# A transformer kernel's memory projection: products with the weights' leading part first, by blocks of rows in the last step only

## The chip, the cores and the metric

The kernel runs on one core of a Trainium2 chip. The metric is the device time of one execution in microseconds (us). Five engines work side by side, each through its own instructions in order: TensorE (PE, with its weight loads PEld), VectorE (DVE), ScalarE (ACT), GpSimd (POOL) and SyncE (SP, which issues DMAs). They wait for each other by semaphores.

## The reference

The program is a two-layer encoder over 512 rows of width 1024, with a memory of 256 rows. Each layer adds to its state, in this order: half a SwiGLU feed-forward block, a mixer, cross-attention to the memory, and half a feed-forward block again. Layer 0's mixer joins a sparse attention over selected keys with a differential attention; layer 1's is a banded attention. The change sits in the projection that gives the cross-attention its keys and values; the memory's part of it does not depend on the state:

```python
def memory_xattn(h, m, wq, wkv, qg, kg, wo):
    q = rmsnorm((h @ wq).reshape(bsz, seq, M_HEADS, M_DIM), qg)
    k, v = jnp.split(m @ wkv, 2, axis=-1)
    k = rmsnorm(k.reshape(bsz, -1, M_HEADS, M_DIM), kg)
    v = v.reshape(bsz, -1, M_HEADS, M_DIM)
    logits = jnp.einsum('bshd,bmhd->bhsm', q, k).astype(jnp.float32) * M_DIM ** -0.5
    p = jax.nn.softmax(logits, axis=-1).astype(v.dtype)
    ...

for layer in range(DEPTH):
    h = h + 0.5 * swiglu(rmsnorm(h, g), wg, wu, wd)
    h = h + mixer(rmsnorm(h, mix_g), ...)
    h = h + memory_xattn(rmsnorm(h, mg), rmsnorm(mem, sg), wq, wkv, qg, kg, wo)
    h = h + 0.5 * swiglu(rmsnorm(h, g), wg, wu, wd)
```

Here `m` is 256 x 1024 and `wkv` 1024 x 1024: the first 512 columns give the keys, the others the values.

## The kernel before, in words

**Split operands.** A float32 product is made of three products in a shorter format. Each operand is split into a leading part (names ending in h) and the rest (names ending in l); x·w becomes xh·wh + xh·wl + xl·wh, added up in one PSUM bank. For weights, `wload` issues the DMA of 128 x 1024 values (wf), ACT makes wh (L161), and DVE or POOL makes wl = wf - wh (L163). `wshare` says which of the two: in layer 0's memory projection POOL makes every second one, in layer 1 DVE all. There are three buffers of wf and two each of wh and wl.

**The memory projection, `mem_kv`.** It has eight steps k, one for each 128 rows of `wkv`. A step loads the weights, loads 128 x 256 values of the memory (`mem`), makes their parts mh (ACT, L1098) and ml (DVE, L1100; two buffers each), and multiplies (L1104). There are four PSUM banks, `banks[c][i]`, with c the half of the columns (0 the keys, 1 the values) and i the block of 128 memory rows. A step is twelve products: for each i, for each c, the three of a split product. After the last step, each i has its keys copied out (ACT, L1110, qk) and its values split (ACT, L1116, and DVE, L1117, vp); then the keys are normed (`head_norm`, L715 sq, L717 ss, L720, L248 on POOL, L724).

**The weaving.** PE's order is that of the code. The projection is part of a generator `gemm` that runs beside the attention's generator `att`. `weave` lets `att` run to its next `yield`, a number of nanoseconds; it then pulls `gemm` until the numbers that `gemm` has yielded cover that gap. The attention's gaps in layer 0 are 3900 after the transposes of a new pair of heads, 600 after each of the two groups of logits, and 1950 ahead of the products with the values (PV); in layer 1, 4550, 600, 2600, and 600 after PV. `mem_kv` yields 1300 after every six products. So a gap of 600 takes six products. The order of the other engines is set by the tile scheduler, from its own estimate of when each instruction can start.

**The attention's lines.** Transposes of q and k (L766, L785; read by ACT L775, L789, L790 and DVE L776, L791), logits (L812), softmax (DVE L825 adds the bias and takes the maximum, ACT L826 the exponential e), transposes of e (L837; read by ACT L840 and DVE L841), PV (L864), its result (ACT L868 ot, DVE L869), and the scaling by the row sums (transposes L873 of POOL's rb, DVE L874). The differential attention ends with sums of squares (L929), a power on POOL (L248, orr), a transpose of it (L937) and DVE L938. Each finished output is split for the next product (ACT L1327 oh, DVE L1329 ol). The logits, transposes and PV share four PSUM banks with the tag pb; all projections share four with the tag pa.

**What follows, `out_proj`.** It multiplies the attention's outputs by the mixer's `w_out` (L657). Its first four banks are those of `mem_kv`, so each has to be emptied first. They are given back by DVE's additions L670 to the next four, before the attention is over.

Of the kernel before, what the change touches and what calls it, by code (L numbers as in the profile page):

```python
# [23 lines left out]
KB = D // P  # L24
# [85 lines left out]
class Encoder:  # L110
# [976 lines left out]
    def mem_kv(self, pre, mp):  # L1087

        nc = self.nc
        gain = self.col(pre + "mem_src_norm")  # L1090
        banks = [[self.bank("pa") for _ in range(2)] for _ in range(2)]
        for k in range(KB):
            wh, wl = self.wload(self.I[pre + "mem_wkv"][k], 1024)
            m = mp.tile([P, NMEM], F32, name="mem", tag="mem", bufs=2)
            nc.sync.dma_start(m, self.I["memT"][k * P:(k + 1) * P, :])
            g = gain[:, k:k + 1]
            mh = mp.tile([P, NMEM], F32R, name="mh", tag="mh", bufs=2)
            nc.scalar.activation(mh, m, AF.Copy, scale=g)  # L1098
            ml = mp.tile([P, NMEM], F32R, name="ml", tag="ml", bufs=2)
            nc.vector.scalar_tensor_tensor(ml, m, g, mh.bitcast(F32), op0=OP.mult, op1=OP.subtract)  # L1100
            for i in range(2):
                for c in range(2):
                    for n, (a, b) in enumerate(((mh, wh), (mh, wl), (ml, wh))):
                        nc.tensor.matmul(banks[c][i], a[:, i * P:(i + 1) * P], b[:, c * 512:(c + 1) * 512],  # L1104
                                         start=(k == 0 and n == 0), stop=(k == KB - 1 and n == 2))
                yield 1300
        kn, vp = [], []
        for i in range(2):
            t = mp.tile([P, S], F32, name="qk", tag="qk", bufs=self.qkbufs)
            nc.scalar.copy(t, banks[0][i])  # L1110
            kn.append(t)
            t = mp.tile([P, 1024], F32R, name="vp", tag="vp", bufs=self.vbufs)
            t3 = t.rearrange("p (h d) -> p h d", d=256)
            p3 = banks[1][i].rearrange("p (h d) -> p h d", d=P)
            r = self.mem_r[:, i:i + 1]
            nc.scalar.activation(t3[:, :, :P], p3, AF.Copy, scale=r)  # L1116
            nc.vector.scalar_tensor_tensor(t3[:, :, P:], p3, r, t3.bitcast(F32)[:, :, :P], op0=OP.mult, op1=OP.subtract)  # L1117
            vp.append(t)
        for i in range(2):
            self.head_norm(kn[i], [self.mem_epsv[:, i:i + 1]], P, mp)  # L1120
        self.memkv = (kn, vp)
# [458 lines left out]
```

## Time and profile before

| quantity | value |
|---|---|
| median of 3 runs | 2075.65 us (2075.44 to 2077.47) |
| profiled execution | 2077.4 us, of which span 2075.6 us, mean granted clock 0.999 |
| busy share PE, PEld, DVE, ACT, POOL | 99%, 88%, 75%, 55%, 17% |
| `mem_kv` products | layer 0: 555.1 to 594.8 us; layer 1: 1572.9 to 1608.9 us |
| one product (L1104) | 390 ns median; 64 of each of the three kinds |

The times of the profile are in us from the start of the span. In a timeline a row has its start, its duration, the engine, the line, the operation, out<-in, partitions x elements and a count, and in brackets the idle time of the engine before it and what ended that. PE's products overlap: one lasts 0.39 us and the next starts 0.23 us after it.

### The profile page before, as it was taken

How to read it: one execution, taken by the hardware profiler on the slowest of the kernel's cores; microseconds unless marked ns; L12 is line 12 of the kernel's file. 1: busy time of each engine (PE TensorE's matmuls, PEld its weight loads, DVE VectorE, ACT ScalarE, POOL GpSimd, SP SyncE). 2: the span in 40 equal slices, each digit the busy share in tenths (PEclk: the TensorE clock that was granted, in tenths of full speed). 3: DMA queues.
4: the chain of work that ended last, by engine and by line, in shares of the span. 5: the costliest groups of instructions: out<-in, count | busy, mean ns of one | idle time of the engine just before them, and what ended most of it. 6: DMA issues, size and time to landing. Idle time of an engine off the chain costs nothing.

```text
span 2075.6 us, 32512 instructions
## 1 busy us (share of the span) xinstructions
PE 2045.8 (99%) x12834; PEld 1825.3 (88%) x12834; DVE 1564.7 (75%) x2246; ACT 1136.6 (55%) x1701; POOL 361.7 (17%) x319
## 2 busy tenths in 40 slices
PE   8999999999999999999999999999999999999999
PEld 7989897888788889898989899988888888989997
DVE  8959687699676698685889687685668687958676
ACT  6636354556686565362556354454778566626442
POOL 1101003345431110000020000013453122000000
PEclk9999999999999999999999999999999999999999
DMA  7837545222241166573556466444223324647643
GB/s 218 221 113 193 142 115 180 82 87 82 83 137 61 62 184 172 143 192 113 128 158 176 129 182 164 122 126 149 92 82 125 100 72 141 184 122 182 164 120 94
DMA packets 86121, 279.65 MB, mean 135 GB/s; under 512 B 9680, under 2 KB 12880, under 8 KB 85968
## 3 DMA queue, kind: packets, MB, share of 16 engines
q1 hardware_dynamic: 74448, 235.62, 35.3%
q0 software_dynamic: 11520, 41.95, 11.8%
q8 instruction: 101, 1.65, 0.3%
q14 instruction: 52, 0.43, 0.1%
HBM read 271.24 MB, written 6.29 MB: 134 GB/s over the span
## 4 chain that ended last, share of the span: by engine, by line
PE 86%; DVE 9%; ACT 2%; issue 2%; POOL 1%; DMA 1%; SPq 0%; DVEq 0%; ACTq 0%; POOLq 0%
PE ps_pa L468 26%; PE ps_pa L604 10%; PE ps_pa L706 10%; PE ps_pb L604 10%; PE ps_pb L468 9%; PE ps_pa L657 4%; PE ps_pb L812 2%; PE ps_pa L323 2%; PE ps_pa L1254 2%; PE ps_pb L864 1%; PE ps_pa L1104 1%; PE ps_pb L657 1%; PE ps_pb L837 1%; DVE wl L163 1%; PE ps_pa L1023 1%
## 5 line engine op out<-in xcount | busy, mean ns | idle before, releaser
L161 ACT ACTIVATE wh<-wf 128x1024 fp32r<-128x1024 f32 (+2 forms) x211 | 215.3, 1022 | 345.9 <-PE ps_pa L604 122.1
L163 DVE TENSOR_TENSOR wl<-wf,wh 128x1024 fp32r<-128x1024 f32 (+2 forms) x169 | 200.0, 1188 | 32.5 <-ACT wh L161 29.9
L446 ACT ACTIVATE wh<-s 128x1024 fp32r<-128x1024 f32 x108 | 114.9, 1063 | 111.9 <-PE ps_pa L468 33.6
L525 POOL DMA_DIRECT2D s<-l_ffn_wq x40 | 35.4, 885 | 782.8 <-ACT s L524 739.0
L447 DVE TENSOR_TENSOR wl<-s,wh 128x1024 fp32r<-128x1024 f32 x108 | 132.0, 1222 | 44.3 <-ACT wh L446 40.1
L446 ACT ACTIVATE wh<-wf 128x1024 fp32r<-128x1024 f32 x84 | 89.2, 1062 | 105.9 <-PE ps_pa L468 32.6
L163 POOL TENSOR_TENSOR wl<-wf,wh 128x1024 fp32r<-128x1024 f32 x42 | 101.4, 2415 | 137.6 <-ACT wh L161 135.7
L706 PE MATMUL ps_pa<-wh,xh 128*128 128x512 f32 x384 | 122.8, 401 | 0.1
L706 PE MATMUL ps_pa<-wh,xl 128*128 128x512 f32 x384 | 119.4, 392 | 0.0
L706 PE MATMUL ps_pa<-wl,xh 128*128 128x512 f32 x384 | 119.1, 391 | 0.0
L447 DVE TENSOR_TENSOR wl<-wf,wh 128x1024 fp32r<-128x1024 f32 x84 | 102.5, 1220 | 5.5 <-PE ps_pa L323 3.0
L228 POOL TENSOR_TENSOR acc<-acc,sq 128x512 f32<-128x512 f32 (+1 forms) x37 | 53.0, 1433 | 260.7 <-ACT sq L227 259.7
L614 DVE TENSOR_TENSOR dn<-ps_pa,R 128x512 f32<-128x512 f32 x48 | 33.1, 689 | 83.9 <-PE ps_pa L604 83.5
L604 PE MATMUL ps_pb<-hh,wh 128*128 128x512 f32 x352 | 95.5, 389 | 0.0
L604 PE MATMUL ps_pb<-hl,wh 128*128 128x512 f32 x352 | 95.4, 389 | 0.0
L604 PE MATMUL ps_pb<-hh,wl 128*128 128x512 f32 x352 | 95.4, 389 | 0.0
L604 PE MATMUL ps_pa<-hh,wh 128*128 128x512 f32 x328 | 88.9, 390 | 0.0
L604 PE MATMUL ps_pa<-hl,wh 128*128 128x512 f32 x328 | 88.7, 389 | 0.0
L604 PE MATMUL ps_pa<-hh,wl 128*128 128x512 f32 x328 | 88.6, 389 | 0.0
L614 DVE TENSOR_TENSOR dn<-ps_pb,R 128x512 f32<-128x512 f32 x48 | 33.0, 687 | 71.1 <-PE ps_pb L604 70.7
L706 PEld LDWEIGHTS ps_pa<-wh,xl 128*128 128x128 f32 x384 | 72.5, 189 | 15.9
L706 PEld LDWEIGHTS ps_pa<-wl,xh 128*128 128x128 f32 x384 | 72.4, 188 | 15.8
(377 smaller groups left out, 5853.1 us busy)
## 6 DMA issues: line engine op xcount, KB each, us to landing
wf<-l_ffn_wq SPq DMA_DIRECT2D x120, 512.0 KB, 3.8
s<-l_ffn_wq SPq DMA_DIRECT2D x80, 512.0 KB, 4.4
s<-l_ffn_wq POOLq DMA_DIRECT2D x80, 512.0 KB, 7.4
wf<-l_ffn_wd SPq DMA_DIRECT2D x64, 512.0 KB, 4.1
wf<-l_w_in SPq DMA_DIRECT2D x48, 512.0 KB, 3.3
wf<-l_ffn_wd SPq DMA_DIRECT2D x32, 384.0 KB, 3.1
wf<-l_mem_wkv SPq DMA_DIRECT2D x16, 512.0 KB, 3.3
wf<-l_w_out SPq DMA_DIRECT2D x16, 512.0 KB, 3.3
```

Of the source, the lines that this page charges most:

```text
L161: self.leading = nc.scalar.activation(wh[:, sl], w[:, sl], AF.Copy)
L163: eng.tensor_sub(wl[:, sl], w[:, sl], wh.bitcast(F32)[:, sl])
L228: self.summed = (eng or nc.gpsimd).tensor_add(acc[:, :n], acc[:, :n], sq[:, :n])
L323: nc.tensor.matmul(p, w[a][:, k * P:(k + 1) * P], xs[k][c], start=k == order[0] and a == c == 0, stop=k == order[-1] and a == 1)
L446: self.leading = nc.scalar.activation(h, t, AF.Copy)
L447: self.parted = nc.vector.tensor_sub(l, t, h.bitcast(F32))
L468: self.nc.tensor.matmul(bank[:, sl], w[a][:, o:o + P], xs[k][b], start=first and z == a == b == k == 0, stop=z == a == 1 and k == KB // 2 - 1,
L604: self.nc.tensor.matmul(bank, w[a][:, j * P:(j + 1) * P], h, start=j == a == e == 0, stop=j == nb - 1 and (a, e) == ops[-1])
L614: nc.vector.tensor_mul(t, bank, f.R)
L657: nc.tensor.matmul(banks[dd], a[:, o:o + P], parts(k)[b], start=k == first and a is wh and b == 0, stop=k == last and a is wl)
L706: nc.tensor.matmul(banks[i], xs[k][a][:, i * P:(i + 1) * P], w[b][:, kk * 512:kk * 512 + 512], start=k == a == b == 0, stop=k == KB - 1 an ...
L812: nc.tensor.matmul(bank[:, o:o + n], a, b[:, :n], start=c == 0, stop=c == len(ops) - 1)
```

## The change: the order of the products within a step

```diff
-            for i in range(2):
+            lead, rest = ((mh, wh), (ml, wh)), ((mh, wl),)
+            for i, ops in ((0, lead), (1, lead), (0, rest), (1, rest)) if k < KB - 1 else ((0, lead + rest), (1, lead + rest)):
                 for c in range(2):
-                    for n, (a, b) in enumerate(((mh, wh), (mh, wl), (ml, wh))):
+                    for a, b in ops:
                         nc.tensor.matmul(banks[c][i], a[:, i * P:(i + 1) * P], b[:, c * 512:(c + 1) * 512],
-                                         start=(k == 0 and n == 0), stop=(k == KB - 1 and n == 2))
-                yield 1300
+                                         start=k == 0 and a is mh and b is wh, stop=k == KB - 1 and b is wl)
+                if i or len(ops) > 1:
+                    yield 1300 if len(ops) > 2 else 870
```

In steps 0 to 6 the eight products with wh come first, four for each block of rows i, and the four with wl follow. `gemm` yields 870 after each of the three groups of four. The last step goes by blocks of rows, six products and 1300 each, with wl last in each half. The instructions are the same in number and kind on every engine; lines behind 1108 have moved by two (L1104 is L1105 now, L1110 is L1112, L1117 is L1119, L1329 is L1331). Beyond the stretches from `mem_kv` to `out_proj` in the two layers the order on every engine is that of before.

The first place is PE in layer 0 where `mem_kv` hands its banks to `out_proj`: L864 is a PV product, L766 and L785 are the transposes for the next pair of heads. Before:

```order
L1104 MATMUL ps_pa<-wl,mh 128x512
L1104 MATMUL ps_pa<-wh,ml 128x512
L864 MATMUL ps_pb<-pz0h,vp 128x512
...
L766 MATMUL ps_pb<-ident,qk 128x128 x4
L785 MATMUL ps_pb<-ident,qk 128x128 x4
L657 MATMUL ps_pa<-oh,wh 128x512
```

And of the change:

```order
L1105 MATMUL ps_pa<-wl,mh 128x512
L864 MATMUL ps_pb<-pz0h,vp 128x512
...
L766 MATMUL ps_pb<-ident,qk 128x128 x4
L785 MATMUL ps_pb<-ident,qk 128x128 x4
L1105 MATMUL ps_pa<-wh,mh 128x512
L1105 MATMUL ps_pa<-wh,ml 128x512
L1105 MATMUL ps_pa<-wl,mh 128x512
```

The last six products of `mem_kv` (the block i = 1) have moved behind PV and the two sets of transposes, and `out_proj` follows on them directly.

The second place is ACT's order at the same point. Before:

```order
L1110 COPY qk<-ps_pa 128x512
L161 ACTIVATE wh<-wf 128x1024
L1116 ACTIVATE vp<-ps_pa,mem_r 128x4x128
L715 ACTIVATE sq<-qk 128x512
L868 COPY ot<-ps_pb 64x512
L775 CAST qz_3577<-ps_pb 64x512
L789 ACTIVATE kz0h<-ps_pb,gcol 64x512
L790 ACTIVATE kz0h<-ps_pb,gcol 64x512
```

And of the change:

```order
L868 COPY ot<-ps_pb 64x512
L775 CAST qz_3577<-ps_pb 64x512
L789 ACTIVATE kz0h<-ps_pb,gcol 64x512
L790 ACTIVATE kz0h<-ps_pb,gcol 64x512
L1112 COPY qk<-ps_pa 128x512
L161 ACTIVATE wh<-wf 128x1024
L1118 ACTIVATE vp<-ps_pa,mem_r 128x4x128
```

The second half's copy, with a weight's wh and the values behind it, has gone from ahead of the attention's four pieces (ot, qz and two halves of k) to behind them.

The third place is DVE, some 20 us later in layer 0, where `out_proj` empties its first four banks (L670). Before:

```order
L670 TENSOR_TENSOR x<-ps_pa,xr 128x512 x2
L890 RECIPROCAL rc<-rs 128x4
L841 TENSOR_TENSOR pz0l<-ps_pb,pz0h 128x512
L841 TENSOR_TENSOR pz1l<-ps_pb,pz1h 128x384
L670 TENSOR_TENSOR x<-ps_pa,xr 128x512
L841 TENSOR_TENSOR pz2l<-ps_pb,pz2h 128x384
L670 TENSOR_TENSOR x<-ps_pa,xr 128x512
L869 TENSOR_TENSOR x<-ps_pb,ot 64x512
```

And of the change:

```order
L890 RECIPROCAL rc<-rs 128x4
L841 TENSOR_TENSOR pz0l<-ps_pb,pz0h 128x512
L841 TENSOR_TENSOR pz1l<-ps_pb,pz1h 128x384
L841 TENSOR_TENSOR pz2l<-ps_pb,pz2h 128x384
L869 TENSOR_TENSOR x<-ps_pb,ot 64x512
L670 TENSOR_TENSOR x<-ps_pa,xr 128x512 x4
```

All four additions have moved behind L869, which waits for PV through ACT's ot.

## The prediction

> **What bounds the kernel now.** I read the page first (busy time and the chain that ended last), then TensorE's waits over the whole run, then the timelines of PE, POOL, DVE and ACT where the changed loop runs: from 555 to 596 us for layer 0 and from 1573 to 1609 us for layer 1, each with the 25 us behind it.
>
> ```profile
> PE 2045.8 (99%) x12834; PEld 1825.3 (88%) x12834; DVE 1564.7 (75%) x2246; ACT 1136.6 (55%) x1701; POOL 361.7 (17%) x319
> PE 86%; DVE 9%; ACT 2%; issue 2%; POOL 1%; DMA 1%; SPq 0%; DVEq 0%; ACTq 0%; POOLq 0%
> ```
>
> TensorE is busy for 2045.8 of 2075.6 us. The change keeps its 192 products and their sizes, so the time can only move by what PE waits. The waits (us in total, times, longest) that touch the loop and what follows it:
>
> ```profile
> PE ps_pb L837 <- DVE qz L776: 2.5, 2, 2.0
> PE ps_pa L1104 <- POOL wl L163: 1.9, 2, 1.0
> PE ps_pa L1104 <- ACT qk L731: 0.7, 1, 0.7
> PE ps_pa L1104 <- DVE wl L163: 0.5, 1, 0.5
> PE ps_pa L657 <- DVE vp L1117: 0.3, 1, 0.3
> ```
>
> Only the second and the fourth are waits on the weights' rest, wl: three waits of 2.4 us together. More than that, the loop has no wait on wl to give back.
>
> **What the change removes.** The three waits on PE's timeline (start, duration, in brackets the idle time and who ended it):
>
> ```profile
> 557.98 0.39 PE L1104 MATMUL ps_pa<-wh,mh 128*128 128x512 f32 x1
> 559.37 0.50 PE L1104 MATMUL ps_pa<-wl,mh 128*128 128x512 f32 x1 [1.01 <-POOL wl L163]
> 559.71 0.39 PE L1104 MATMUL ps_pa<-wh,ml 128*128 128x512 f32 x1
> ...
> 560.17 0.39 PE L1104 MATMUL ps_pa<-wl,mh 128*128 128x512 f32 x1
> 560.40 0.40 PE L1104 MATMUL ps_pa<-wh,ml 128*128 128x512 f32 x1
> 560.64 0.60 PE L937 MATMUL ps_pb<-ident,orr 128*128 128x128 f32 x4
> ...
> 579.99 0.50 PE L1104 MATMUL ps_pa<-wl,mh 128*128 128x512 f32 x1 [0.90 <-POOL wl L163]
> ...
> 1600.57 0.50 PE L1104 MATMUL ps_pa<-wl,mh 128*128 128x512 f32 x1 [0.55 <-DVE wl L163]
> ```
>
> Products start 0.23 us apart (560.17, 560.40). From 557.98 to 559.37 is 1.39, so 1.16 is lost, and the product behind starts 0.34 later instead of 0.23: a restart costs 0.11. The first wait cost 1.27; the others, by the same 0.15 beside the idle time, 1.05 + 0.11 = 1.16 and 0.70 + 0.11 = 0.81. Each wl would now be wanted eight products (1.8 us) after its step begins rather than one or two, which covers all three. Removed: 3.24 us.
>
> **What it adds: the attention's turns.** The loop is woven with the attention by the numbers it yields. A gap of 600 between two groups of logits now takes four products (0.92 us) where it took six (1.38 us); so the same step ends later in the attention's course, and what PE meets there is met earlier against the other engines. I go through the places in time order; "t" is PE's own time at the place.
>
> *First attention block, L937.* PE would now reach L937 at 560.64 - 1.27 less two products (16 stand ahead of it, not 18): 558.91. Its operand orr comes from POOL:
>
> ```profile
> 538.42 2.37 POOL L163 TENSOR_TENSOR wl<-wf,wh 128x1024 fp32r<-128x1024 f32 x1 [1.30 <-ACT wh L161]
> ...
> 556.94 2.38 POOL L163 TENSOR_TENSOR wl<-wf,wh 128x1024 fp32r<-128x1024 f32 x1
> 559.29 1.00 POOL L248 TENSOR_TENSOR orr<-ov,mhalf 128x4 f32<-128x4 f32 x1
> ...
> 584.13 2.38 POOL L163 TENSOR_TENSOR wl<-wf,wh 128x1024 fp32r<-128x1024 f32 x1 [4.20 <-ACT wh L161]
> ```
>
> orr is behind that very wl and ends at 560.29, plus 0.05 to start as between POOL's 559.32 and PE's 559.37. L937 starts at 560.35, only 0.29 earlier than before, with two products (0.46) still owed: a wait of 1.44, with its restart 1.55, so that the gain of 1.27 becomes a loss of 0.28. Bounds of the added wait: 0 (orr ahead of wl on POOL) to 1.6.
>
> *Transposes of layer 0 after 587 us.* The four rests now stand between the two groups of logits, so the buffer of wl comes free later, and POOL's 2.4 us of splitting start at about the time of DVE's split of the outputs. What that does has a pair of rows:
>
> ```profile
> 539.17 2.17 DVE L1329 TENSOR_TENSOR ol<-x,oh 128x512 fp32r<-128x512 f32 x1
> ...
> 587.67 0.69 DVE L1329 TENSOR_TENSOR ol<-x,oh 128x512 fp32r<-128x512 f32 x1
> ```
>
> The first lay over POOL's row of 538.42 (to 540.79) and ended at 541.34, its last 0.55 alone; the second ran alone. The Trainium skill, SBUF — State Buffer, section "Who interferes with whom", says that a DVE instruction with two SBUF inputs contends with a GpSimd instruction reading SBUF; the rows agree (2.17 against 0.69 us).
>
> The split can be 1.48 us longer, and the softmax's first pass (L825) stands behind it, whose logits' banks the transposes L837 want. Bounds 0 and 1.48; I take 0.8, about the middle, as part of it is DVE's slack.
>
> *Handover to the output projection, layer 0.* The last step's second half (six products) is pushed behind the PV products and the next pair's transposes, and its bank must be emptied before out_proj's fourth bank is written.
>
> ```profile
> 595.83 0.28 PE L864 MATMUL ps_pb<-pz2l,vp 128*128 128x256 f32 x1
> ...
> 596.74 0.48 PE L657 MATMUL ps_pa<-oh,wh 128*128 128x512 f32 x1
> ...
> 598.89 0.39 PE L657 MATMUL ps_pa<-oh,wh 128*128 128x512 f32 x1
> ```
>
> ```profile
> 594.98 0.62 ACT L1110 COPY qk<-ps_pa 128x512 f32<-128x512 f32 x1
> 595.44 1.11 ACT L161 ACTIVATE wh<-wf 128x1024 fp32r<-128x1024 f32 x1
> 596.40 0.73 ACT L1116 ACTIVATE vp<-ps_pa,mem_r 128x512 fp32r<-128x512 f32 x1
> ...
> 597.67 0.58 ACT L868 COPY ot<-ps_pb 64x512 f32<-64x512 f32 x1
> 598.28 0.58 ACT L775 CAST qz<-ps_pb 64x512 fp32r<-64x512 f32 x1
> 598.76 0.68 ACT L789 ACTIVATE kz0h<-ps_pb,gcol 64x512 fp32r<-64x512 f32 x1
> 599.46 0.68 ACT L790 ACTIVATE kz0h<-ps_pb,gcol 64x512 fp32r<-64x512 f32 x1
> ```
>
> ```profile
> 597.16 0.75 DVE L1117 SCALAR_TENSOR_TENSOR vp<-ps_pa,mem_r,vp 128x512 fp32r<-128x512 f32 x1 [0.71 <-ACT vp L1116]
> ```
>
> With t the start of the last PV product: PE reaches the fourth bank at t + 0.91 (595.83 to 596.74) + 6 x 0.23 + 2.15 (596.74 to 598.89) = t + 4.44. ACT has its four attention pieces ahead now: ot starts at t + 0.37 (618.17 to 618.54, below), then 0.61 + 0.48 + 0.70 + 0.70, the copy 0.46, wh 0.96, vp 0.76, and DVE's 0.75 behind: t + 5.79. The wait is 1.35, with its restart 1.46. Bounds 0 and 1.5.
>
> *out_proj's second four banks, layer 0.* The four additions L670 that empty the first four now all stand behind L869 on DVE; before, all four ran ahead of it.
>
> ```profile
> 618.17 0.28 PE L864 MATMUL ps_pb<-pz2l,vp 128*128 128x256 f32 x1
> ```
>
> ```profile
> 618.54 0.58 ACT L868 COPY ot<-ps_pb 64x512 f32<-64x512 f32 x1 [1.81 <-PE ps_pb L864]
> ```
>
> ```profile
> 616.56 0.68 DVE L670 TENSOR_TENSOR x<-ps_pa,xr 128x512 f32<-128x512 f32 x1
> ...
> 619.16 0.68 DVE L869 TENSOR_TENSOR x<-ps_pb,ot 64x512 f32<-64x512 f32 x1 [1.92 <-ACT ot L868]
> ```
>
> From t = 618.17, L869 starts at t + 0.99 and takes 0.68, L670 0.68: the bank is free at t + 2.35. PE wants it at t + 0.91. Wait 1.44, with restart 1.55; bounds 0 and 1.6. The later three banks follow at 0.68 each, three products (0.69) apart.
>
> *Layer 1.* Its first step waits for a bank, and its end for another:
>
> ```profile
> 1576.95 0.50 PE L1104 MATMUL ps_pa<-wh,mh 128*128 128x512 f32 x1 [0.68 <-ACT qk L731]
> ...
> 1613.87 0.51 PE L657 MATMUL ps_pa<-oh,wh 128*128 128x512 f32 x1 [0.28 <-DVE vp L1117]
> ```
>
> The bank of 1576.95 is the fourth; six products now stand ahead of it instead of nine, while ACT's copy comes no earlier: +0.69 (bounds 0 and 0.7). Between two groups of logits and their transposes PE has four products of cover less (0.92), of which the softmax's slack takes a part I cannot see: +0.5 (bounds 0 and 0.92). At the handover ACT has vp and sq (0.73 and one like it) ahead of the last two exponentials, so the transposes wait: +0.5; and the second half's qk, wh and vp stand behind the next group's exponentials, with DVE's own wl ahead of L1117, so the wait of 1613.87 (0.28, in all 0.45) grows. Adding these pieces up in the new order gives about +1.45 net; bounds for the two together -0.45 (it goes) and 2.6.
>
> **Sum.** Removed 3.24. Added in layer 0: 1.55 + 0.8 + 1.46 + 1.55 = 5.36. Layer 1: 0.69 + 0.5 + 1.95 = 3.14. Net +5.3 us: the profiled execution's 2077.4 (span 2075.6) would become 2082.7. That execution lies 1.75 above the median of 2075.65, so the forecast is 2075.65 + 5.3 = **2080.9 us**. With every added term at its lower bound the sum is -3.7, at its upper 1.55 + 1.5 + 1.5 + 1.6 + 0.7 + 0.9 + 2.6 - 3.24 = +7.1; a stretch at the lower clock (below) adds 1.7.
>
> **The rivals.**
>
> *The covers hold.* Only the waits on wl vanish: ACT and DVE drain the banks in time since they too start 3 us earlier. -3.2 and -0.45 give 2072.0 to 2072.4, inside 0.2% (4.15 us, about what a measurement here can tell from no change). For it: ACT is idle 45% of the span. Against: PE is moved nearer to engines whose queue order, not their speed, sets the wait. It decides where POOL's orr and the two handover banks are ready.
>
> *The waits merely change place.* L937's wait takes the place of the first and the layer-1 bank's of the third, and DVE's and ACT's new queue order at the handovers costs half of what I put down (1.5 of 3.0 in layer 0, 0.7 of 1.95 in layer 1): -3.24 + 1.55 + 0.8 + 1.5 + 0.69 + 0.7 = +2.0, so 2077.7: no change that can be told.
>
> *A long wait lowers the granted clock.* After the wait of 2.0 on qz (542.2) PE ran slower:
>
> ```profile
> 542.20:544.20 2.00, 1.99 (x7) 1.71 (x8) 1.97 (x4) 0.48 (x1) 0.00 (x0) 0.58 0.62 234
> 544.20:546.20 2.00, 2.00 (x6) 1.53 (x6) 0.30 (x1) 0.00 (x0) 0.00 (x0) 0.57 0.03 8
> ```
>
> The columns end with the granted clock, 0.58 and 0.57, and the DMA's two: 4 us at 0.575 lose 1.7 us of work. Should two of my waits run together to 2 us (the handover's could), the sum is 5.3 + 1.7 = +7.0: 2082.7. TensorE: Matmul & The Clock Gate in the Trainium skill, Part 1, has the clock fall only after an idle window of about 3.4 us; by it no wait here would do that, and the sum stays. The row, with 2.05 us, speaks against so long a bound.
>
> **How the numbers follow.** New waits outweigh the old ones, 0.50; with the lower clock too, 0.14; waits change place, 0.24; covers hold, 0.12. The first includes sums from +3 on, so slower by over 0.2% gets 0.14 + about 0.46 = 0.60; faster by over 0.2% needs the last case and 0.5 us beyond it: 0.05; within 0.2% the rest, 0.35. The range reaches from 2075.0 (the rival without change, its handover terms near nothing) to 2085.5 (the lower clock and half of the remaining upper bounds); the likeliest case alone spans 2078.5 to 2083.
>
> **What would show it.** Right: no wait of the product line on wl; L937 waiting about 1.4 for POOL's orr; L657 waiting for vp and for x (L670), over 1 us each in layer 0; the fourth bank in layer 1 waiting about 1.4. Every stretch outside 555 to 625 and 1573 to 1620 us unchanged. Wrong: waits on wl still there, L657 in layer 0 without a wait, or PE's products themselves longer than 390 ns.

## The result, and the profile after

The change takes a median of 2086.88 us (2083.55 to 2088.4, 6 runs) against 2075.55 us before (2073.9 to 2077.47, 6 runs). The ratio is 1.0051 with an interval of 1.0041 to 1.0061, that is +10.6 us (8.5 to 12.7). The forecast was 2080.9 us, +5.3, with 2085.5 as the upper end of its range: the sign and most of the places were right, the size was half, and the median lies above the range.

The profiled execution took 2085.28 us, with a span of 2083.4. From its page, the busy times and the chain:

```profile
PE 2048.4 (98%) x12830; PEld 1824.0 (88%) x12834; DVE 1568.3 (75%) x2246; ACT 1136.4 (55%) x1701; POOL 363.7 (17%) x319
PE 87%; DVE 9%; ACT 2%; issue 1%; POOL 0%; DMA 0%; SPq 0%; DVEq 0%; ACTq 0%
```

TensorE's busy time rose by 2.6 us and the span by 7.8; the rest is waiting. Of TensorE's waits over the run, these are the ones that the change touches (total us, times, longest):

```profile
PE ps_pa L657 <- DVE vp L1119: 2.6, 2, 1.4
...
PE ps_pa L1105 <- ACT qk L731: 1.4, 1, 1.4
PE ps_pb L937 <- POOL orr L248: 1.3, 1, 1.3
...
PE ps_pa L657 <- DVE x L670: 1.2, 1, 1.2
PE ps_pb L837 <- DVE m L825: 1.1, 2, 0.6
...
PE ps_pb L812 <- DVE x L869: 1.0, 1, 1.0
...
PE ps_pb L864 <- DVE pz0l L841: 0.7, 1, 0.7
```

No product of `mem_kv` waits for wl any more. In place of those waits the attention, `out_proj` and `mem_kv` itself wait for seven other things. The same waits in their places on PE's timeline, layer 0 first:

```profile
559.28 0.65 PE L937 MATMUL ps_pb<-ident,orr 128*128 128x128 f32 x4 [1.32 <-POOL orr L248]
...
570.21 0.50 PE L864 MATMUL ps_pb<-pz0l,vp 128*128 128x512 f32 x1 [0.70 <-DVE pz0l L841]
...
589.98 0.93 PE L837 MATMUL ps_pb<-ident,e 128*128 128x128 f32 x6 [0.61 <-DVE m L825]
...
601.34 0.50 PE L657 MATMUL ps_pa<-oh,wh 128*128 128x512 f32 x1 [1.36 <-DVE vp L1119]
...
621.77 0.50 PE L657 MATMUL ps_pa<-oh,wh 128*128 128x512 f32 x1 [1.17 <-DVE x L670]
...
1580.57 0.50 PE L1105 MATMUL ps_pa<-wh,mh 128*128 128x512 f32 x1 [1.36 <-ACT qk L731]
...
1587.56 0.50 PE L812 MATMUL ps_pb<-kz0h,qz 128*128 128x512 f32 x1 [0.96 <-DVE x L869]
...
1592.31 0.94 PE L837 MATMUL ps_pb<-ident,e 128*128 128x128 f32 x6 [0.45 <-DVE m L825]
...
1618.28 0.98 PE L837 MATMUL ps_pb<-ident,e 128*128 128x128 f32 x7 [0.38 <-DVE vp L1119]
...
1622.59 0.47 PE L657 MATMUL ps_pa<-oh,wh 128*128 128x512 f32 x1 [1.26 <-DVE vp L1119]
```

Where the span grew follows from four instructions that both programs have at the same place of the order (starts on PE's timeline, us):

| instruction | before | after | after - before |
|---|---|---|---|
| L929, ahead of layer 0's `mem_kv` | 554.31 | 553.22 | -1.09 |
| L323, first product of the block after layer 0's mixer and cross-attention | 728.29 | 732.34 | +4.05 |
| L766, ahead of layer 1's `mem_kv` | 1542.78 | 1546.40 | +3.62 |
| L323, the same in layer 1 | 1736.00 | 1743.93 | +7.93 |

Layer 0 lost 5.14 us and layer 1 lost 4.31, together 9.45; the stretches without a moved instruction differ by -1.09, -0.43 and -0.1 between these two executions. The forecast for the two was +2.9 (5.36 added, 2.43 removed) and +2.3 (3.14 and 0.81).

### The profile page after: what moved, and what is told of

Its sections match the earlier page's. It is cut to its first block, busy times and chain, and to the rows that moved or that the text cites. A ratio compares the mean times of both kernels' runs of the same rounds, so it can differ in the third digit from the quotient of the medians.

```text
span 2083.4 us, 32505 instructions
## 1 busy us (share of the span) xinstructions
PE 2048.4 (98%) x12830; PEld 1824.0 (88%) x12834; DVE 1568.3 (75%) x2246; ACT 1136.4 (55%) x1701; POOL 363.7 (17%) x319
## 4 chain that ended last, share of the span: by engine, by line
PE 87%; DVE 9%; ACT 2%; issue 1%; POOL 0%; DMA 0%; SPq 0%; DVEq 0%; ACTq 0%
PE ps_pa L468 26%; PE ps_pa L604 10%; PE ps_pa L706 10%; PE ps_pb L604 10%; PE ps_pb L468 9%; PE ps_pa L657 4%; PE ps_pa L323 3%; PE ps_pb L812 2%; PE ps_pa L1256 2%; PE ps_pb L864 2%; PE ps_pa L1105 1%; PE ps_pb L657 1%; PE ps_pb L837 1%; DVE wl L163 1%; PE ps_pa L1023 1%
```

## The experiments

All are compared with the kernel before on the same chip. A time in us is the ratio's difference times 2075 to 2076.

**Each layer alone.** The change with `if pre == "l0_"` around it, or `"l1_"`, and the old loop otherwise:

```diff
+            if pre == "l0_":
+                lead, rest = ((mh, wh), (ml, wh)), ((mh, wl),)
...
+            else:
+                for i in range(2):
...
```

> The change in layer 0 only; layer 1 as before. By the two traces layer 0's mixer takes 5.1 us of the 9.4 that the two mixers lost in them: +5.1 us against the kernel before, with the waits on orr, pz0l, the softmax, vp and x as in the change. If what the layers lose depends on each other, or if the time lies outside the mixers, another number.

> The change in layer 1 only; layer 0 as before. By the two traces +4.3 us against the kernel before; with the run above it adds up to the whole change (+10.6 by its ratio, 9.4 by the traces' two mixers). A sum well below that would say that part of the time is neither layer's.

Measured: layer 0 alone 2080.72, ratio 1.0024 (1.0015 to 1.0033), +5.0 us; layer 1 alone 2081.19, ratio 1.0026 (1.0016 to 1.0036), +5.4 us. They add up to +10.4 where the whole change has +10.6, each known to about 2 us. So each layer loses by itself, and no loss outside them is needed to make the sum. The waits in the two profiles are not all those of the change: layer 0 alone waits 2.36 for orr and not for pz0l, and layer 1 alone waits 2.12 where the change waits 1.26 for vp.

**Turns and order apart.** The change does two things: it orders the products of a step anew, and it lets the attention in after every four products. e1_turns does the second alone, e2_order the first:

```diff
 # e1_turns: the order of before
+            every = [(i, c, a, b) for i in range(2) for c in range(2) for a, b in ((mh, wh), (mh, wl), (ml, wh))]
+            for n, (i, c, a, b) in enumerate(every):
...
+                if k < KB - 1 and n % 4 == 3:
+                    yield 870
+                elif k == KB - 1 and n % 6 == 5:
+                    yield 1300
 # e2_order: the order of the change
+            every = [(i, c, a, b) for ops in (lead, rest) for i in range(2) for c in range(2) for a, b in ops]
+            if k == KB - 1:
+                every = [(i, c, a, b) for i in range(2) for c in range(2) for a, b in lead + rest]
...
+                if n % 6 == 5:
+                    yield 1300
```

> The old order of the twelve products (wh, wl, wh for each bank), but the attention gets its turns after every four products, as in the change; the last step by sixes. Theory A (the turns cost: the attention is met earlier against the other engines, and the last six products slip behind PV): about +8 to +11 us on the kernel before, since the waits on wl stay as well; the waits of out_proj's products on vp and on x in layer 0 (1.36 and 1.17 us in the change) appear here too, with products of the old order. Theory B (the order itself costs: wl's buffers are held to the end of the step, so that its next split starts late and meets other work on VectorE): 0 to +2 us, and no wait on vp or x above 0.5 us in layer 0.

> The changed order (eight products with wh first, then four with wl; the last step by blocks of rows), but the attention gets its turns after every six products, as before the change. Theory A: the three waits on wl go and little else comes, -1 to -3.3 us against the kernel before. Theory B: most of the loss is still there, +5 to +9 us, with PV waiting for pz0l (0.70 us in the change) and the transposes for the softmax (0.61 us).

Measured: the turns alone 2082.87, ratio 1.0033 (1.0021 to 1.0045), +6.9 us; the order alone 2079.64, ratio 1.002 (1.0011 to 1.0028), +4.2 us. Neither theory got both, and both times fell short of the loss that was expected: each half costs, and the two add up to 11.1 us where the whole has 10.6. The largest waits tell which is whose. With the turns alone (PE's timeline):

```profile
557.88 0.50 PE L1103 MATMUL ps_pa<-wl,mh 128*128 128x512 f32 x1 [1.01 <-POOL wl L163]
...
599.69 0.50 PE L657 MATMUL ps_pa<-oh,wh 128*128 128x512 f32 x1 [1.36 <-DVE vp L1119]
...
620.11 0.50 PE L657 MATMUL ps_pa<-oh,wh 128*128 128x512 f32 x1 [1.17 <-DVE x L670]
...
1586.02 0.50 PE L812 MATMUL ps_pb<-kz0h,qz 128*128 128x512 f32 x1 [0.87 <-DVE x L869]
...
1619.84 0.50 PE L657 MATMUL ps_pa<-oh,wh 128*128 128x512 f32 x1 [1.17 <-DVE vp L1119]
```

With the order alone (PE's timeline):

```profile
558.50 0.65 PE L937 MATMUL ps_pb<-ident,orr 128*128 128x128 f32 x4 [1.92 <-POOL orr L248]
...
584.14 0.50 PE L812 MATMUL ps_pb<-kz0h,qz 128*128 128x512 f32 x1 [0.69 <-DVE x L869]
...
1576.28 0.50 PE L1106 MATMUL ps_pa<-wh,mh 128*128 128x512 f32 x1 [1.37 <-ACT qk L731]
...
1589.96 0.98 PE L837 MATMUL ps_pb<-ident,e 128*128 128x128 f32 x7 [0.65 <-ACT e L826]
...
1602.80 0.50 PE L1106 MATMUL ps_pa<-wh,ml 128*128 128x512 f32 x1 [0.76 <-DVE ml L1100]
```

The two handover waits of layer 0, 1.36 and 1.17, are the turns' to the hundredth. The waits on orr and on layer 1's fourth bank are the order's. The rest does not divide so: the change's 0.70 on pz0l and 0.61 on the softmax in layer 0 stand in neither half's profile, and the order alone waits 0.69 for x and 0.76 for ml where the change does not. That the two times add up so well is therefore partly chance. The order, which was meant to give 3.24 us, costs 4.2 when the turns are left alone: what was waiting for wl now waits for the next late thing.

**GpSimd's splits.** In layer 0 GpSimd makes every second wl of this projection. e5_ws gives all to VectorE, in the change; e7_before_ws does the same to the kernel before. The edit reaches further than the projection: the share stays set while `out_proj` loads its weights, so four of its splits move to VectorE as well. In the change GpSimd makes eight wl between 555 and 662 us, four of them for `out_proj`; in e5_ws it makes none. The same holds for the three runs further down that have this edit.

```diff
-WS = (2, 3, 0, 1, 1, 2, 1, 2, 0, 0, 3, 2, 1, 1, 0, 3)
+WS = (2, 3, 0, 1, 1, 2, 1, 0, 0, 0, 3, 2, 1, 1, 0, 3)
```

> The change, but in layer 0's memory projection VectorE makes every wl (GpSimd made every second one). Theory C (in layer 0 the order costs where GpSimd's 2.4 us of wl run beside VectorE's ml and ol and ahead of orr): the waits on orr (1.32), pz0l (0.70) and the softmax (0.61) go, with their restarts about 4 us; the waits on vp (1.36) and x (1.17) stay. So about +6.5 us on the kernel before, where the whole change has +10.6. Rival D (VectorE is the bound there, and four splits of 1.2 us more bring as much back): +9 us or more, with waits on wl from VectorE in place of those.

> The kernel before, with VectorE making every wl of layer 0's memory projection. A control for the two runs beside it. If GpSimd's lateness is all there is, the two waits of 1.01 and 0.90 us go: -2.4 us. If VectorE has no room there, waits on VectorE's wl take their place: 0 to +2 us.

Measured: e7_before_ws 2075.3, ratio 0.9997 (0.9988 to 1.0006), no change that can be told: the waits of 1.01 and 0.90 on wl are gone, and one of 0.62 on pz0l and one of 0.28 on qz came in their place. e5_ws 2086.54, ratio 1.0056 (1.004 to 1.0071), +11.6 us: no gain either, where theory C had +6.5. Its waits on PE's timeline, though, did what theory C says:

```profile
557.52 0.65 PE L937 MATMUL ps_pb<-ident,orr 128*128 128x128 f32 x4 [0.30 <-POOL orr L248]
...
578.85 0.44 PE L864 MATMUL ps_pb<-pz1l,vp 128*128 128x384 f32 x1 [0.17 <-DVE pz1l L841]
...
598.42 0.47 PE L657 MATMUL ps_pa<-oh,wh 128*128 128x512 f32 x1 [2.47 <-DVE vp L1119]
```

orr fell from 1.32 to 0.30, pz0l's 0.70 is gone (the 0.17 on pz1l is at the next pair's PV), and so is the softmax's 0.61. But the wait on vp grew from 1.36 to 2.47, and TensorE ran on at a lower clock. Its windows (length of the window; PE's busy time and count; granted clock; the DMA engines' busy share and GB/s):

```profile
598.00:600.00 2.00, 1.58 (x7) 0.78 0.63 186
600.00:602.00 2.00, 2.00 (x10) 0.50 0.19 76
602.00:604.00 2.00, 2.00 (x10) 0.87 0.00 0
```

VectorE's rows say why vp was later:

```profile
595.92 1.69 DVE L163 TENSOR_TENSOR wl<-wf,wh 128x1024 fp32r<-128x1024 f32 x1 [0.82 <-ACT wh L161]
597.54 0.74 DVE L1119 SCALAR_TENSOR_TENSOR vp<-ps_pa,mem_r,vp 128x512 fp32r<-128x512 f32 x1
```

One of the splits that GpSimd makes in the change, at 600.00 us and for `out_proj`, now stands right ahead of vp's second half. So the waits that C named go, and what they gave is lost again at the handover. The rival D had the size of the time, but no wait on VectorE's wl came, as it had said.

**The handover.** Does the slip of six products behind PV make the waits on vp and x? e6_join and e9_align let the second half of the last step follow sooner:

```diff
 # e6_join: no turn behind the last four products of step 6
-                if i or len(ops) > 1:
+                if (i or len(ops) > 1) and not (k == KB - 2 and len(ops) == 1):
 # e9_align: the first half of the last step yields 100
-                    yield 1300 if len(ops) > 2 else 870
+                    yield 870 if len(ops) < 3 else 1300 if i else 100
```

> The change, but the last four products of step 6 yield nothing, so that the first half of the last step is pulled together with them and the second half comes ahead of PV again. Theory A' (the handover's waits come from the six products that slipped behind PV): the waits on vp and x in layer 0 go (1.6 and 1.5 us with restarts), the one on vp in layer 1 shrinks; about -3 to -4.5 us against the change, +6 to +7.5 on the kernel before. Rival E (whatever position the last products have, ACT's or VectorE's queue is late there): the waits stay above 1 us each and the time stays at +10.

> The change, but the first half of the last step yields 100 instead of 1300, so that its second half follows at once and out_proj's banks are handed over at the same place of the attention as before the change, in both layers (the run that joined step 6 to the last step moved them in layer 1 only). Theory A': the waits on vp (1.36) and x (1.17) in layer 0 go, layer 1's on vp and e shrink: with restarts about 3.2 + 2 us less than the change, +5 to +6 us on the kernel before. Rival E (ACT's or VectorE's queue is late there wherever the products stand): above 1 us of wait each remains, +9 us or more.

Measured: e6_join 2084.57, ratio 1.004 (1.0027 to 1.0054), +8.3 us. In layer 0 the edit moved no product (the gap ahead of PV, 1950, was covered with or without the turn), and both waits stood as before, 1.35 and 1.17; in layer 1, where products did move, the wait on vp fell from 1.26 to 0.49. So it tested layer 1 only, and the expectation for layer 0 was wrong about the edit. e9_align moved them in both: 2081.65, ratio 1.003 (1.0018 to 1.0041), +6.2 us. In layer 0 neither vp nor x is waited for; what is left there, and layer 1's vp, on PE's timeline:

```profile
560.66 0.65 PE L937 MATMUL ps_pb<-ident,orr 128*128 128x128 f32 x4 [2.36 <-POOL orr L248]
...
591.84 0.93 PE L837 MATMUL ps_pb<-ident,e 128*128 128x128 f32 x6 [0.62 <-DVE m L825]
...
1620.27 0.50 PE L657 MATMUL ps_pa<-oh,wh 128*128 128x512 f32 x1 [1.00 <-DVE vp L1119]
```

Layer 0's two handover waits are the slip's, and the rival E is out for them. Layer 1's is so in part only. The wait on orr, 1.32 in the change, was 2.36 in this execution, with the same instructions ahead of it; the section on the hardware takes that up.

e10_align_ws puts e9_align and VectorE's splits together:

> The run above with every wl of layer 0's projection on VectorE. Theory C with the handover out of the way: the waits on orr, pz0l and the softmax go as they did with VectorE alone, and this time nothing is given back at the handover: 2.5 to 4 us less than the run above, +1.5 to +3 us on the kernel before. If VectorE's four splits more move the loss elsewhere again: no less than the run above.

Measured: 2078.15, ratio 1.0011 (1.0002 to 1.002), +2.3 us, 3.9 less than e9_align. With the handover out of the way, taking GpSimd's splits away pays about what was expected of e5_ws. The two intervals overlap a little, so the 3.9 is known only roughly. Its waits by line, those of the change among them:

```profile
PE ps_pa L1105 <- ACT qk L731: 1.4, 1, 1.4
...
PE ps_pa L657 <- DVE vp L1119: 1.0, 1, 1.0
...
PE ps_pb L812 <- DVE x L869: 1.0, 1, 1.0
...
PE ps_pb L837 <- DVE m L825: 0.4, 1, 0.4
...
PE ps_pb L937 <- POOL orr L248: 0.3, 1, 0.3
...
PE ps_pb L864 <- DVE pz1l L841: 0.2, 1, 0.2
```

The first four are all in layer 1: 3.74 us of waits there against 1.51 (0.68, 0.55, 0.28) before. In layer 0 the two at the end and one of 0.21 on qz are left.

**The change again.** The same kernel profiled and timed a second time, beside e9_align and e10_align_ws.

> The change itself, profiled and timed again. Its runs lay from 2083.6 to 2088.4 us and its profiled one (2085.3) 1.6 us under their median. If the rest is the granted clock, this profile shows a stretch at a lower clock behind one of the new waits when its time is near 2088, and none when it is near 2083.5; if it is something else, the waits themselves differ between the two profiles by more than 1 us.

Measured: 2084.11 (2083.27 to 2087.43), ratio 1.0046 (1.0031 to 1.0062), +9.5 us; its profiled execution took 2083.27. It has the waits of the first profile to within 0.11 (orr 1.32, pz0l 0.59, the softmax 0.61, vp 1.36, x 1.17; in layer 1 1.36, 0.97, 0.44, 0.38, 1.28) and no stretch at a lower clock inside the run; the first, at 2085.28, had one at 541 us. That fits the clock as what parts these two executions, near 2083.3 and near 2085.3. No profile of the change at 2088 was taken, so what adds the rest there is not shown.

**Is there something in the order?** e8_mid uses it away from the places where it was found to cost, in steps 1 to 6, with turns after six products and VectorE's splits; e12_layer0_mid does so in layer 0 only (its condition has `or pre == "l1_"` as well, and the products by banks are in the order of before).

```diff
+            every = [(i, c, a, b) for ops in (lead, rest) for i in range(2) for c in range(2) for a, b in ops]
+            if k in (0, KB - 1):
+                every = [(i, c, a, b) for i in range(2) for c in range(2) for a, b in lead + rest]
...
+                if n % 6 == 5:
+                    yield 1300
```

> Leading parts first in steps 1 to 6 only (the first and the last step by blocks of rows, so that the fourth bank in layer 1 is reached after nine products again), the attention's turns after six products as before, and every wl of layer 0's projection on VectorE. If the losses of the order are the three places named (the early fourth bank, orr behind GpSimd's wl, GpSimd's wl beside VectorE): -1 to -3 us against the kernel before. If holding the buffers of wl to the end of a step costs by itself: +1 to +3 us, with waits on ml, on the softmax or on x in both layers.

> Leading parts first in steps 1 to 6 of layer 0 alone, turns after six products, every wl of that projection on VectorE; layer 1 is the kernel before. By the profile of the run with both layers, what layer 0 still waits for in the mixer is 0.46 and 0.24 us, against 1.01 and 0.90 before, and layer 1 loses nothing: -1.5 us (-0.5 to -2.5), too little to be told from no change in one comparison.

Measured: e8_mid 2076.19, ratio 1.0002 (0.9993 to 1.0011); e12_layer0_mid 2075.45, ratio 1.0 (0.9991 to 1.0009). Neither can be told from the kernel before, and no run is faster. The expected -1 to -3 and -1.5 were not seen, though the intervals do not exclude a gain of 1.5. Layer 1's early fourth bank is gone in e8_mid (0.68 again), but in layer 1 it waits 0.72 for x and 0.76 for ml. In e12_layer0_mid layer 0 waits 0.41 and 0.24 us where it waited 1.01 and 0.90, so about 1.3 us are there by the profile, less than the comparison can show.

## Why the prediction was wrong in size

Point by point, in the order of its parts.

**What bounds the kernel, and what is removed:** right. PE's waits moved the time, and all three waits on wl went.

**L937 on orr, layer 0:** predicted 1.44 of idle time, measured 1.32. With the restart the row of 559.28 lies 1.48 behind its place, against 1.55. Some luck is in this: e9_align and e3_layer0, with the same instructions up to there, waited 2.36.

**Transposes on the softmax, layer 0:** predicted 0.8, measured about 0.8 with what lies around the idle 0.61. The mechanism is the one named; that the size agrees is luck, since 0.8 was the middle of its bounds. GpSimd's split, and VectorE's ol beside it:

```profile
586.33 2.41 POOL L163 TENSOR_TENSOR wl<-wf,wh 128x1024 fp32r<-128x1024 f32 x1 [7.91 <-PE ps_pa L1105]
```

```profile
586.54 2.75 DVE L1331 TENSOR_TENSOR ol<-x,oh 128x512 fp32r<-128x512 f32 x1
```

ol took 2.75 us here, and 0.69 when it ran alone in the kernel before.

**Handover, layer 0:** predicted 1.35 on vp and 1.44 on x, measured 1.36 and 1.17. e9_align confirms the cause: without the slip both are gone.

**Layer 1's bank:** predicted +0.69, measured 1.36 - 0.68 = 0.68; e2_order says it belongs to the order. **Layer 1's cover:** 0.5 predicted, 0.45 measured in the place named (the transposes), where the kernel before had 0.11. **Layer 1's handover:** +1.95 predicted for the two pieces, measured 0.19 + 0.38 + 1.26 - 0.28 = 1.55 of idle time, an estimated 1.8 to 1.9 with restarts.

So each wait that was in the sum came within about 0.3 us of its term. **The step that failed is the list itself: "I go through the places in time order" left out places, which the sum thereby put at nothing.** Two are large.

The first is PV in layer 0, which waits for pz0l; it was in neither the sum nor a rival. The wait of 570.21 and the late rows behind it cost 1.1 us, and the next pair's PV at 581 another 0.5 (one split of 1.22 us by VectorE between pz0l and pz1l). The rows of GpSimd and of VectorE at the first of them:

```profile
566.87 2.40 POOL L163 TENSOR_TENSOR wl<-wf,wh 128x1024 fp32r<-128x1024 f32 x1
```

```profile
567.75 1.80 DVE L1100 SCALAR_TENSOR_TENSOR ml<-mem,cols,mh 128x256 fp32r<-128x256 f32 x1 [0.22 <-ACT mh L1098]
569.47 0.68 DVE L841 TENSOR_TENSOR pz0l<-ps_pb,pz0h 128x512 fp32r<-128x512 f32 x1
...
578.19 0.51 DVE L1100 SCALAR_TENSOR_TENSOR ml<-mem,cols,mh 128x256 fp32r<-128x256 f32 x1
```

The memory's ml, 0.51 us at 578.19, takes 1.80 beside GpSimd's split, and pz0l stands behind it; in the kernel before ml came after the three splits of this PV (pz0l at 569.10, ml at 570.64). It is the mechanism that the prediction had found for ol and then looked for in one place only. e5_ws, where the wait is gone, supports it; e7_before_ws shows that VectorE's own split can make the same wait, 0.62.

The second is the logits of layer 1 that wait for L869 (0.96, about 1.0 with the restart). Two things meet there. PE comes after four products where it came after six: e1_turns, with the same turns, waits 0.87. And VectorE is later, by the same mechanism once more. Its rows ahead of L869 in the change, which run beside GpSimd's norming of the keys (L724, from 1584.23):

```profile
1584.60 1.26 DVE L1100 SCALAR_TENSOR_TENSOR ml<-mem,cols,mh 128x256 fp32r<-128x256 f32 x1
1585.79 1.00 DVE L720 TENSOR_SCALAR ss<-ss,epsv 128x8 f32<-128x8 f32 x1
```

L720 takes 1.0 us there in the kernel before too. But ml takes 0.48 in that kernel and 0.47 in e1_turns, where it stands ahead of wl and ends before L724 begins. e8_mid, with the old turns and an ml of 1.27, waits 0.72. So either is enough for most of the wait, and the change has both. The prediction gave the lost cover of four products one wait, of 0.5; there were two.

Together these places cost about 2.7 of the 4.2 us by which 9.45 exceeds 5.3. The rest is in places of about 0.4 us or less each, found by comparing every start-to-start time with the usual one of its form: layer 1's PV products behind their own late rows (0.4 and 0.3), a product of layer 1's loop behind ml (0.35), changes from a group of products to the attention in layer 0 (0.2 each or less), and the edges of the wait on vp in layer 0 (about 0.25).

**The last 1.2 us** (10.6 against 9.45) lie within the interval, and the second comparison gave +9.5. The granted clock bears this out in part. Among the ten runs of the change two have a mean clock of 1.000: 2083.55 and 2083.27 us. The second is 9.4 above the median (2073.87) of the twelve runs with 1.000 of the kernel before that were taken beside it. By this, what exceeds about 9.4 goes with a lower clock. Behind new waits over 2 us the clock was seen to fall in e4_layer1, e5_ws and e9_align, which hold parts of this change; so the mechanism of the rival with the lower clock is real. In the change's own two profiles the new waits stayed under 1.4 and drew none; whether it acts in the runs near 2088 is not shown.

**The range.** Its upper end of 2085.5 follows from the profiled execution's 2077.4 (5.3 + 1.7 + 0.9 more is 2085.3). From the median, on which the forecast itself is built, the same sum gives 2083.6.

**The other rivals.** The covers did not hold, which e2_order says most clearly: with the old turns, other waits take the place of those on wl and cost more than they did. "The waits merely change place" was too cheap by the same list. "New waits outweigh the old ones" was the right case.

## What to carry to other kernels

Where one engine is 99% busy and the others run in fixed orders behind it, a wait that goes lets that engine meet the next late result sooner: price an edit by what every queue delivers at the new times, all of them, and not by the wait that it removes. A mechanism found at one place (here GpSimd and VectorE, one of them slower while both run) is to be looked for at every place where the same pair overlaps, before and after. And a yield that steers a weave is a change of its own: the order and the turns cost 4.2 and 6.9 us here when each was changed alone.

## What the runs showed of the hardware

**Which of two engines was slowed went with a start 0.02 us earlier.** In the change's profile GpSimd's orr and VectorE's wl start together (POOL's rows, then DVE's):

```profile
558.20 1.02 POOL L248 TENSOR_TENSOR orr<-ov,mhalf 128x4 f32<-128x4 f32 x1
```

```profile
558.20 1.29 DVE L163 TENSOR_TENSOR wl<-wf,wh 128x1024 fp32r<-128x1024 f32 x1
559.42 1.26 DVE L1100 SCALAR_TENSOR_TENSOR ml<-mem,cols,mh 128x256 fp32r<-128x256 f32 x1
```

orr takes its 1.02 us and VectorE's ml, 0.47 elsewhere, takes 1.26. In e9_align, with the same instructions up to there:

```profile
558.55 2.06 POOL L248 TENSOR_TENSOR orr<-ov,mhalf 128x4 f32<-128x4 f32 x1
```

```profile
558.53 1.21 DVE L163 TENSOR_TENSOR wl<-wf,wh 128x1024 fp32r<-128x1024 f32 x1
559.66 0.47 DVE L1100 SCALAR_TENSOR_TENSOR ml<-mem,cols,mh 128x256 fp32r<-128x256 f32 x1
```

VectorE started 0.02 ahead; orr took 2.06, and PE waited 2.36 for it instead of 1.32. e3_layer0 and e2_order had the second outcome too, again with VectorE 0.02 ahead (orr took 2.06 in both); e6_join and e11_again had the first, with equal starts (1.02). The Trainium skill, SBUF — State Buffer, section "Who interferes with whom", has it that the order of issue decides who blocks; the profiles with VectorE 0.02 ahead agree, and in the others the two starts are equal to the hundredth, so that the order cannot be read.

**A wait of 2.05 us was followed by a lower granted clock in half of the executions.** In all fourteen profiles TensorE waits 2.05 to 2.06 us for qz near 541 us, in a stretch that no kernel here altered. In seven the granted clock over 542 to 547 us was then 0.66 to 0.82, in the other seven 1.00. Where it fell, about 1.7 us of work were lost, for instance 5 x 0.34 in the kernel before. Behind new waits it fell after 2.12 (e4_layer1, where the change waits for vp), 2.36 (e9_align, on orr) and 2.47 us (e5_ws, on vp), not after 2.36 (e3_layer0, on orr), and after none under 2 us. The Trainium skill, TensorE: Matmul & The Clock Gate, Part 1, has a window of about 3.4 us that runs by itself, and a fall after an idle one; the measurement differs in that waits of 2.05 us were enough in half of the cases, and fits in that the same wait does it in one execution and not in the next.
